# One load at a step: rows of x for the norms and the next tile's transposed x in the input projections of a hybrid decoder layer

## The chip, the core and the metric

The kernel runs on one core of a Trainium2 chip. The core has five engines with a queue of instructions each: TensorE (PE; its weight loads are shown apart, as PEld), VectorE (DVE), ScalarE (ACT), GpSimd (POOL) and SyncE (SP), which here issues nearly all transfers (DMAs) to the core's 16 DMA engines. An engine works its queue off in order, and an instruction waits until what it reads is there and the buffer that it writes is free. The metric is the device time of one execution in microseconds (us), as the median of several runs.

## The reference

One decoder layer on x of 2048 rows and 1024 columns, in float32: an input projection that feeds attention in a sliding window and a convolution group side by side, an output projection of both, and a gated feed-forward part. Every part has an RMS norm ahead of it and one behind.

```python
hn = rms_norm(h, mix_pre_g)                # 2048 x 1024
proj = hn @ w_in                           # 1024 x 1792: q, k, v, and u of the conv group
attn_out = sliding_window_attention(q, k, v, attn_sinks, rel_bias)   # window 128, 8 heads, 2 kv heads
conv_out = conformer_conv(u, ...)          # glu, causal depthwise conv of width 31, layer norm, swish, w_conv_pw
mixed = concatenate([attn_out, conv_out]) @ w_out
h = h + rms_norm(mixed, mix_post_g)
hn = rms_norm(h, ffn_pre_g)
ff = (silu(hn @ w_gate) * (hn @ w_up)) @ w_down      # 1024 -> 2816 -> 1024
h = h + rms_norm(ff, ffn_post_g)
```

`rms_norm(x, g)` divides each row by the root of its mean square: that root is what the rows of x are loaded for below.

## The kernel before

**Tiles and stages.** The 2048 rows are cut into four tiles of 512. A stage has a letter, and names of tiles in the profile carry it: `mm@A` is a PSUM bank of the input projections, `x@A` a tile of x, `hl@W` one of the output projection. A0 to A3 are the input projections of the four tiles, B attention, C the conv taps on DVE and their tail, U the product of `w_conv_pw` and `w_out`, W the output projection, H and F the norm and the gate/up matmuls of the feed-forward part, G the product with `w_down`, X the table of the relative-position bias. Float32 products are made of three fp32r matmuls: each operand is split into a high part (ACT, L127) and a rest (POOL, L129, or DVE, L94), and `three` multiplies high by high, high by rest and rest by high.

**Input projections.** One tile takes 14 units, one for each 128 of the 1792 columns of `w_in`. A unit loads its weights (`raw@A<-w_in`, L137, 512 KB; tile 0 stores the rests to `lo_in`, L131, and the other tiles load them from there, L126), splits them and runs 24 matmuls of 128x512 over the eight 128-row pieces of the transposed x (`hl@A`, `mid@A`, `chl@A`). After unit u, `step(u)` calls `hooks[u]`, if there is one: that is where the next tile is made ready.

**Getting the next tile ready.** Four functions do it. `load_x` (L247) loads the transposed x of a tile in four pieces of 512 KB (`x@A<-xT`, L252). `row_norms` (L261) loads rows of x, 128 at a time (`p@A<-x` or `hl@A<-x`, L266, 512 KB), has ACT square and sum each (`junk`, L267), and makes the reciprocal roots from the sums with one `rsqrt`, some small instructions on DVE and POOL (tiles `sm@A`). `norm_x` (hooks h2 and h3) turns the roots into a row that lies along the columns (`gb@A<-ident`, transposes into a bank, a copy by ACT), and `split_x` (h4 and h5) multiplies and splits x into the operands of the next tile. Tile 1 gets its own row norms during A0; those of tiles 2 and 3 are made together during A1. Tiles of x lie in a pool of four buffers (`x`), rows in pools of four (`p`) or eight (`hl`), weights in two (`raw`) and six (`w`). `yt` is a single buffer, used by the conv tail (`yt@C`) and then by the output projection (`yt@W`).

**What sets the order.** The units are written by a loop (`run`). Between its pieces, lanes (attention `lb`, taps `lc`, fold `lu`, output projection `lw` and others) are pumped by credits in proportion to the cost of each piece, so the order in which code is written mixes all stages. Behind that, a scheduler puts each engine's instructions in an order of its own: among what its model holds ready, the instruction written first goes first. Conv taps carry extra ties to the projections' instructions (`dve`), so that they keep pace. So a hook that is written differently can move instructions of other stages too, on every engine.

Of the kernel before, what the change touches and what calls it, by code (L numbers as in the profile page):

```python
# [17 lines left out]
AF = mybir.ActivationFunctionType  # L18
# [5 lines left out]
D = 1024  # L24
DFF = 2816
P = 128
T = 512
# [10 lines left out]
def layer_kernel(ctx, tc, x, xT, cols, rows, sinks, relb, onehot, w_in, w_pw, w_out, w_gate, w_up, w_down, out):  # L38
    nc = tc.nc
# [7 lines left out]
    lab = ["X0"]  # L47

    def nm(s):
        uid[0] += 1  # L50
        return f"{s}@{lab[0]}_{uid[0]}"
# [6 lines left out]
    def f4(tag, shape=(P, D)):  # L58
        return t_(tag, shape)
# [19 lines left out]
    act = nc.scalar.activation  # L79
# [64 lines left out]
    def rsqrt(ssq, n, mean_over, beside_taps=True):  # L144
        v = sm(n)
        y = sm(n)
        t = sm(n)
        vts(v, ssq, 1.0 / mean_over, EPS, ALU.mult, ALU.add)
        vts(y.bitcast(I32), v.bitcast(I32), 1, None, ALU.logical_shift_right)
        vts(y.bitcast(I32), y.bitcast(I32), -1, 0x5F3759DF, ALU.mult, ALU.add)  # L150
        for _ in range(3):
            if beside_taps:
                ptt(t, y, y, ALU.mult)
                ptt(t, t, v, ALU.mult)
                nc.gpsimd.tensor_scalar(t, t, -0.5, 1.5, ALU.mult, ALU.add)
# [45 lines left out]
    for i in range(4):  # L201
        xt = f4("x", (P, 2, T))
# [34 lines left out]
    junk = cst.tile([P, D], BF16, name="junk")  # L237
# [18 lines left out]

    rn = {}

    def row_norms(ts, tag):
        lab[0] = f"A{ts[0]}"  # L260
        n = 4 * len(ts)  # L261
        ssq = sm(n)
        for i in range(n):
            xt = f4(tag)
            r0 = ts[0] * T + i * P
            nc.sync.dma_start(xt, x[r0 : r0 + P])  # L266
            act(junk, xt, AF.Square, accum_out=ssq[:, i : i + 1])  # L267
# [16 lines left out]
    def norm_x(t, xs, acc):  # L284
        lab[0] = f"A{t}"
        bank_of = mm if t else ct
        if t:
            r = acc
        else:
            o = bank_of()  # L290
            for s in range(4):
                mat(o[:, s : s + 1], acc[:, s * P : (s + 1) * P], ones, start=True, stop=True)
            r = rsqrt(o[:, 0:4], 4, D, False)
        dg = f2("gb")
        for s in range(4):
            vts(dg[:, s * P : (s + 1) * P], ident, 0.0, r[:, s : s + 1], ALU.mult, ALU.add)
        yield
        lab[0] = f"A{t}"
        o = bank_of()
        for s in range(4):  # L300
            nc.tensor.transpose(o[:, s * P : (s + 1) * P], dg[:, s * P : (s + 1) * P], ident)
        rb = f2("gb")
        act(rb, o, AF.Copy)
        yield rb
# [1026 lines left out]
    H1, H2, H3, H4 = 0, 4, 7, 11  # L1331
# [28 lines left out]
    xa = {}  # L1360
# [8 lines left out]
    for t in range(NT):  # L1369
        hooks = {}  # L1370
        if t + 1 < NT:

            def h1(t=t + 1):
                xa[t] = load_x(t)

            def h3(t=t + 1):
                xa[t][2] = next(xa[t][2])

            def h4(t=t + 1):
                hn_a[t] = split_x(t, xa[t][0], xa[t][2], range(4))  # L1380
# [7 lines left out]
            def h2(t=t + 1):  # L1388
                xa[t] += [rn[t], norm_x(t, xa[t][0], rn[t])]
                next(xa[t][2])  # L1390
# [107 lines left out]
```

## Time and profile before

| | |
|---|---|
| median of 3 runs | 1985.41 us (1983.29 to 1989.4) |
| the profiled execution | 1988.67 us |
| its span, first to last instruction | 1986.6 us |
| mean granted clock of TensorE | 0.992 |
| PE busy | 1930.2 us (97%) |
| PEld busy | 1542.3 us (78%) |
| DVE busy | 1460.2 us (73%) |
| ACT busy | 955.2 us (48%) |
| POOL busy | 336.4 us (17%) |

The last matmul of the input projections starts at 484.5 us; the gate/up stage takes about 620 to 1010 us, the `w_down` products of the first half up to about 1340, and the second half of the feed-forward part the rest. In the rows of the profile, a time in brackets is idle time of the engine just before an instruction, followed by what ended it. `SPq` is an instruction of SP's queue that issues a DMA: its time is that of the issue, and the transfer lands later. In a row of a stretch stand, after its length, the busy time of PE, PEld, DVE, ACT and POOL with the number of instructions, then the granted clock of TensorE, the busy share of the DMA engines and GB/s.

### The profile page before, as it was taken

What the parts mean: (1) busy time and instruction counts of PE and PEld (TensorE: products, weight loads), DVE (VectorE), ACT (ScalarE), POOL (GpSimd) and SP (SyncE); (2) the same over time, 40 slices, a digit from 0 to 9 for tenths busy, and PEclk for the clock granted to TensorE, in tenths of its full rate; (3) what the DMA queues carried; (4) which work ended last, traced back from release to release, by engine and by line L of the source; (5) the groups of instructions that cost most, each with busy time, mean ns of one, the idle gap of its engine ahead of it and who ended that gap; (6) DMA issues with size and microseconds to landing.
All of it is one profiled execution on the core that took longest, in us unless ns stands there. A gap on an engine that the chain in (4) does not pass through costs nothing.

```text
span 1986.6 us, 26669 instructions
## 1 busy us (share of the span) xinstructions
PE 1930.2 (97%) x8730; PEld 1542.3 (78%) x8730; DVE 1460.2 (73%) x2578; ACT 955.2 (48%) x1878; POOL 336.4 (17%) x415
## 2 busy tenths in 40 slices
PE   8999999998999999899999999989999999999997
PEld 6777767776777778778888778768888888888886
DVE  5999969986875898888658975766666665455557
ACT  5455454436737633334355466556634433345443
POOL 4011111003121200000000110144423332311003
PEclk9999999999999999999999999989999999999999
DMA  8797757669659867885477788797844542466664
GB/s 312 253 316 234 228 176 242 213 198 306 203 191 353 290 216 237 285 267 181 154 236 251 266 302 282 270 315 244 289 149 165 170 164 81 143 232 194 210 196 144
DMA packets 229403, 454.56 MB, mean 229 GB/s; under 512 B 22632, under 2 KB 48400, under 8 KB 229264
## 3 DMA queue, kind: packets, MB, share of 16 engines
q1 hardware_dynamic: 211024, 426.64, 64.5%
q10 hardware_dynamic: 18240, 26.22, 3.6%
q8 instruction: 69, 1.13, 0.2%
q14 instruction: 70, 0.57, 0.1%
HBM read 331.65 MB, written 121.12 MB: 228 GB/s over the span
## 4 chain that ended last, share of the span: by engine, by line
PE 43%; DMA 10%; DVE 9%; issue 3%; POOL 2%; ACT 2%; SPq 1%; DVEq 0%; ACTq 0%; POOLq 0%
PE mm@F L85 29%; PE mm@G L85 12%; DVE fc@C L94 2%; PE tr@W L85 2%; DMA gb@F<-keeps 1%; DVE hl@G L94 1%; DMA mids<-fa@F 1%; DMA fa@G<-mids 1%; DMA td<-fc@G 1%; DVE w@F L94 1%; DMA fc@G<-w_down 1%; DMA wx@G<-w_down 1%; DVE fa@F L94 1%; DVE chl@F L94 1%; DMA mixT<-fc@C 1%
## 5 line engine op out<-in xcount | busy, mean ns | idle before, releaser
L94 DVE SCALAR_TENSOR_TENSOR fc@C<-glu@C,colt,fc@C 128x512 f32<-128x512 f32 x480 | 356.5, 760 | 2.9
L85 PE MATMUL mm@F<-hl@H,w@F 128*128 128x512 f32 x1056 | 253.0, 390 | 3.3 <-ACT mm@F L919 2.0
L85 PE MATMUL mm@G<-hl@G,hl@G 128*128 128x512 f32 x924 | 232.6, 397 | 11.2 <-ACT hl@G L792 7.7
L85 PEld LDWEIGHTS mm@F<-hl@H,w@F 128*128 128x128 f32 x1056 | 197.5, 188 | 46.3 <-ACT mm@F L919 3.7
L85 PEld LDWEIGHTS mm@G<-hl@G,hl@G 128*128 128x128 f32 x924 | 173.0, 190 | 51.7 <-ACT hl@G L792 9.0
L85 PE MATMUL mm@A<-hl@A,w@A 128*128 128x512 f32 x840 | 206.5, 395 | 4.2 <-ACT w@A L127 1.9
L792 ACT ACTIVATE w@F<-chl@F 128x512 fp32r<-128x512 f32 x220 | 135.4, 625 | 142.1 <-PE mm@F L85 131.5
L85 PE MATMUL mm@G<-w@G,hl@G 128*128 128x512 f32 x876 | 199.4, 389 | 0.0
L85 PEld LDWEIGHTS mm@G<-w@G,hl@G 128*128 128x128 f32 x876 | 164.4, 188 | 34.1
L85 PEld LDWEIGHTS mm@A<-hl@A,w@A 128*128 128x128 f32 x840 | 155.4, 188 | 42.2 <-ACT w@A L127 2.6
L94 DVE TENSOR_TENSOR w@F<-chl@F,w@F 128x512 fp32r<-128x512 f32 x198 | 144.8, 735 | 35.9 <-ACT w@F L792 35.3
L85 PE MATMUL mm@F<-ql@H,w@F 128*128 128x512 f32 x528 | 128.4, 391 | 9.2 <-ACT mm@F L1026 5.0
L85 PE MATMUL mm@F<-mid@H,w@F 128*128 128x512 f32 x528 | 131.7, 396 | 0.0
L85 PE MATMUL mm@F<-p@H,w@F 128*128 128x512 f32 x528 | 129.4, 390 | 0.0
L85 PE MATMUL mm@F<-x@H,w@F 128*128 128x512 f32 x528 | 125.7, 391 | 0.0
L85 PEld LDWEIGHTS mm@F<-ql@H,w@F 128*128 128x128 f32 x528 | 98.8, 188 | 31.6 <-ACT mm@F L1026 6.4
L494 POOL TENSOR_SCALAR_AFFINE_SELECT p@B<-p@B 128x512 f32<-128x512 f32 x62 | 57.6, 938 | 374.0 <-ACT p@B L492 372.7
L85 PEld LDWEIGHTS mm@F<-mid@H,w@F 128*128 128x128 f32 x528 | 100.0, 190 | 21.9 <-ACT fa@F L1047 0.5
L85 PEld LDWEIGHTS mm@F<-p@H,w@F 128*128 128x128 f32 x528 | 99.5, 188 | 21.0 <-ACT at@F L1040 0.2
L85 PEld LDWEIGHTS mm@F<-x@H,w@F 128*128 128x128 f32 x528 | 98.6, 188 | 21.5 <-issue 0.8
L127 ACT ACTIVATE w@A<-raw@A 128x512 fp32r<-128x512 f32 x110 | 67.4, 625 | 93.5 <-PE mm@A L85 54.8
L94 DVE TENSOR_TENSOR w@G<-raw@G,w@G 128x512 fp32r<-128x512 f32 x73 | 51.5, 705 | 68.1 <-ACT w@G L792 66.8
(302 smaller groups left out, 3300.6 us busy)
## 6 DMA issues: line engine op xcount, KB each, us to landing
mids<-fa@F SPq DMA_DIRECT2D x154, 256.0 KB, 2.8
raw@A<-w_in SPq DMA_DIRECT2D x55, 512.0 KB, 4.7
w@A<-lo_in SPq DMA_DIRECT2D x84, 256.0 KB, 3.6
fc@G<-mids SPq DMA_DIRECT2D x77, 256.0 KB, 3.5
fa@G<-mids SPq DMA_DIRECT2D x75, 256.0 KB, 4.6
gb@F<-keeps SPq DMA_DIRECT2D x72, 256.0 KB, 3.9
w@W<-fold SPq DMA_DIRECT2D x32, 512.0 KB, 5.1
chl@F<-w_gate SPq DMA_DIRECT2D x22, 512.0 KB, 4.1
```

The lines of the kernel that those rows point to most:

```text
L85: r = nc.tensor.matmul(*args, **kw)
L94: r = op(*args, **kw)
L127: act(w[:, 0], raw, AF.Copy)
L494: nc.gpsimd.affine_select(out=pg[:, kb].rearrange("p (i q) -> p i q", q=P), in_=pg[:, 1].rearrange("p (i q) -> p i q", q=P), compare_op=AL ...
L792: act(w[:, 0], x, AF.Copy)
```

## The change

The hooks load less at once. `load_x` takes a number of pieces and adds them to the tile's list; `row_norm` loads and squares one piece of 128 rows and makes the `rsqrt` of a tile with its fourth. Each tile has its own `rsqrt` now, with 4 values in place of 8 for tiles 2 and 3. During A0 the pieces of x go with steps 2, 3, 8 and 9, and the rows of tile 1 with steps 4 to 7, where all four of x stood at step 2 and all rows at step 4. During A1 the pieces of x go with steps 0, 1, 7 and 8, the rows of tile 2 with steps 2 to 5 and those of tile 3 with steps 6 to 9, where four of x stood at step 0 and eight rows at step 2; `h2` of tile 2 moves from step 7 to step 6. During A2 nothing changes: four of x at step H1.

```diff
-    def load_x(t):
+    def load_x(t, xs, n):
         lab[0] = f"A{t}"
-        xs = []
-        for i in range(4):
+        for i in range(len(xs), len(xs) + n):
             xt = f4("x", (P, 2, T))
             nc.sync.dma_start(xt, xT[2 * i : 2 * i + 2, :, t * T : (t + 1) * T].rearrange("c p t -> p c t"))
             xs.append(xt)
         started.add(f"x{t}")
-        return [xs]
...
-    def row_norms(ts, tag):
-        lab[0] = f"A{ts[0]}"
-        n = 4 * len(ts)
-        ssq = sm(n)
-        for i in range(n):
-            xt = f4(tag)
-            r0 = ts[0] * T + i * P
-            nc.sync.dma_start(xt, x[r0 : r0 + P])
-            act(junk, xt, AF.Square, accum_out=ssq[:, i : i + 1])
-        r = rsqrt(ssq, n, D)
-        for j, t in enumerate(ts):
-            rn[t] = r[:, 4 * j : 4 * j + 4]
+    def row_norm(t, i, tag):
+        lab[0] = f"A{t}"
+        if i == 0:
+            rn[t] = sm(4)
+        xt = f4(tag)
+        r0 = t * T + i * P
+        nc.sync.dma_start(xt, x[r0 : r0 + P])
+        act(junk, xt, AF.Square, accum_out=rn[t][:, i : i + 1])
+        if i == 3:
+            rn[t] = rsqrt(rn[t], 4, D)
...
-            def h1(t=t + 1):
-                xa[t] = load_x(t)
...
-            def h0(t=t + 1):
-                row_norms([t] if t == 1 else [2, 3], "p" if t == 1 else "hl")
+            xa[t + 1] = [[]]
+
+            def hx(n, t=t + 1):
+                load_x(t, xa[t][0], n)
+
+            def hr(t, i):
+                row_norm(t, i, "p" if t == 1 else "hl")
...
             if t == 0:
-                hooks = {2: h1, 4: h0, 8: h2, 10: h3, 11: h4, 12: h5}
+                hooks = {2: at_(hx, 1), 3: at_(hx, 1), 4: at_(hr, 1, 0), 5: at_(hr, 1, 1), 6: at_(hr, 1, 2), 7: at_(hr, 1, 3)}
+                hooks.update({8: lambda: (hx(1), h2()), 9: at_(hx, 1), 10: h3, 11: h4, 12: h5})
             elif t == 1:
-                hooks = {0: h1, 2: h0, 7: h2, 9: h3, 10: h4, 11: h5}
+                hooks = {0: at_(hx, 1), 1: at_(hx, 1)}
+                hooks.update({2 + i: at_(hr, 2, i) for i in range(4)})
+                hooks.update({6: lambda: (hr(3, 0), h2()), 7: lambda: (hx(1), hr(3, 1)), 8: lambda: (hx(1), hr(3, 2))})
+                hooks.update({9: lambda: (hr(3, 3), h3()), 10: h4, 11: h5})
             else:
-                hooks = {H1: h1, H2: h2, H3: h3, H4: h4}
+                hooks = {H1: at_(hx, 4), H2: h2, H3: h3, H4: h4}
```

Lines from L270 to L1365 of the kernel before are four lower in the changed one (L301 is L297 there). The scheduler's order of both kernels shows where instructions stand. On SP, in the first tile, the rows from the last pieces of x on, before (`lo_in` is a store of rests, `glu_scr` a store of the conv group's input, `glu@C` its load, `onehot` and `b_scr` belong to the bias table):

```order
L252 DMA x@A_46_339<-xT 128x2x512
L137 DMA raw@A_47_341<-w_in 128x1024
L131 DMA lo_in<-w@A_33_272 128x512
L616 DMA wx@U_366_2300<-w_pw 128x2x512
L131 DMA lo_in<-w@A_34_276 128x512
L137 DMA raw@A_55_395<-w_in 128x1024
L131 DMA lo_in<-w@A_48_343 128x512
L131 DMA lo_in<-w@A_49_347 128x512
L137 DMA raw@A_70_477<-w_in 128x1024
```

And the same place now:

```order
L137 DMA raw@A_44_335<-w_in 128x1024
L251 DMA x@A_100_710<-xT 128x2x512
L131 DMA lo_in<-w@A_33_272 128x512
L612 DMA wx@U_370_2319<-w_pw 128x2x512
L131 DMA lo_in<-w@A_34_276 128x512
L137 DMA raw@A_53_391<-w_in 128x1024
L131 DMA lo_in<-w@A_45_337 128x512
L131 DMA lo_in<-w@A_46_341 128x512
L137 DMA raw@A_62_446<-w_in 128x1024
```

The fourth piece of x stands behind the weights of unit 3 instead of ahead of them; the three pieces before it, and tile 1's rows, stand where they stood. Further on in the same tile, the loads of the bias table: before,

```order
L137 DMA raw@A_83_571<-w_in 128x1024
L356 DMA glu_scr<-fa@A_51_376 128x512
L131 DMA lo_in<-w@A_76_523 128x512
L131 DMA lo_in<-w@A_77_527 128x512
L137 DMA raw@A_90_621<-w_in 128x1024
L657 DMA b_scr<-fa@X_54_386 8x256
L538 DMA glu@C_88_614<-glu_scr 128x512
L131 DMA lo_in<-w@A_84_573 128x512
L131 DMA lo_in<-w@A_85_577 128x512
L137 DMA raw@A_96_670<-w_in 128x1024
L666 DMA mb@X_61_438<-b_scr 128x8x128
```

and now:

```order
L137 DMA raw@A_77_546<-w_in 128x1024
L534 DMA glu@C_82_589<-glu_scr 128x512
L131 DMA lo_in<-w@A_69_495 128x512
L653 DMA b_scr<-fa@X_51_380 8x256
L131 DMA lo_in<-w@A_70_499 128x512
L137 DMA raw@A_88_617<-w_in 128x1024
L662 DMA mb@X_59_434<-b_scr 128x8x128
```

`raw@A_83` and `raw@A_77` are the weights of the same unit (the eighth), `raw@A_90` and `raw@A_88` those of the ninth: the store to `b_scr` and the load of `mb@X` stand one unit of weights earlier.

On PE, at the end of the fourth tile's projections (`ct@C<-ident,yt@C` are the last transposes that read the conv tail's `yt`, `tr@B<-kz,ql@A` the scores of attention), before:

```order
L85 MATMUL mm@A_769_4719<-mid@A_504_3192,w@A_767_4713 128x512 x3
L85 MATMUL mm@A_769_4719<-mid@A_505_3196,w@A_767_4713 128x512 x2
L601 MATMUL ct@C_613_3763<-ident,yt@C_543_3430 128x128 x4
L85 MATMUL mm@A_769_4719<-mid@A_505_3196,w@A_767_4713 128x512
L85 MATMUL mm@A_769_4719<-mid@A_506_3200,w@A_767_4713 128x512 x3
L85 MATMUL mm@A_769_4719<-mid@A_507_3204,w@A_767_4713 128x512 x3
L85 MATMUL mm@A_769_4719<-hl@A_520_3295,w@A_768_4716 128x512 x3
L85 MATMUL mm@A_769_4719<-hl@A_521_3299,w@A_768_4716 128x512 x3
L85 MATMUL mm@A_769_4719<-hl@A_522_3303,w@A_768_4716 128x512 x3
L85 MATMUL mm@A_769_4719<-hl@A_523_3307,w@A_768_4716 128x512 x3
L85 MATMUL tr@B_783_4778<-kz,ql@A_752_4594 128x256
```

and now:

```order
L85 MATMUL mm@A_773_4738<-mid@A_508_3211,w@A_771_4732 128x512 x3
L85 MATMUL mm@A_773_4738<-mid@A_509_3215,w@A_771_4732 128x512 x3
L85 MATMUL mm@A_773_4738<-mid@A_510_3219,w@A_771_4732 128x512 x3
L597 MATMUL ct@C_617_3782<-ident,yt@C_547_3449 128x128 x4
L85 MATMUL mm@A_773_4738<-mid@A_511_3223,w@A_771_4732 128x512 x3
L85 MATMUL mm@A_773_4738<-hl@A_524_3314,w@A_772_4735 128x512 x3
L85 MATMUL mm@A_773_4738<-hl@A_525_3318,w@A_772_4735 128x512 x3
L85 MATMUL mm@A_773_4738<-hl@A_526_3322,w@A_772_4735 128x512 x3
L85 MATMUL mm@A_773_4738<-hl@A_527_3326,w@A_772_4735 128x512 x3
L85 MATMUL tr@B_787_4797<-kz,ql@A_756_4613 128x256
```

The transposes stand four matmuls later in the unit: 19 follow before the scores in the one, 15 in the other.

Orders differ in single rows up to the end of the gate/up stage, agree in the `w_down` products behind it, and differ at a few places after those. One such place on SP, in the gate/up stage (`chl@F<-w_gate` is a load of gate weights, `td<-` stores partial products of the first half, `gb@F<-keeps` loads kept products), before:

```order
L966 DMA raw@F_1357_8119<-w_up 128x1024
L968 DMA chl@F_1343_8002<-w_gate 128x1024
L1085 DMA td<-wx@G_1334_7956 128x512
L1085 DMA td<-fc@G_1336_7958 128x512
L1054 DMA mids_4750<-fa@F_1298_7717 128x512
L998 DMA gb@F_1339_7981<-keeps_4755 128x512
L1079 DMA wx@G_1367_8169<-w_down 128x512
```

and now:

```order
L962 DMA raw@F_1361_8138<-w_up 128x1024
L1081 DMA td<-wx@G_1338_7975 128x512
L1081 DMA td<-fc@G_1340_7977 128x512
L1075 DMA wx@G_1371_8188<-w_down 128x512
L964 DMA chl@F_1347_8021<-w_gate 128x1024
L1050 DMA mids_4769<-fa@F_1302_7736 128x512
L994 DMA gb@F_1343_8000<-keeps_4774 128x512
```

The gate weights stand behind two stores and a load of `w_down` that stood behind them.

More of the change, by code (lines that the diff above doesn't have):

```diff
@@ L1371, in layer_kernel, with h2 @@
         if t + 1 < NT:
-            def h1(t=t + 1):
-                xa[t] = load_x(t)
+            xa[t + 1] = [[]]
[3 more added lines that the diff above has]
+                row_norm(t, i, "p" if t == 1 else "hl")
+            def h2(t=t + 1):
+                xa[t] += [rn[t], norm_x(t, xa[t][0], rn[t])]
+                next(xa[t][2])
             def h3(t=t + 1):
@@ L1383, in h5 @@
                 hn_a[t] += split_x(t, xa[t][0], xa[t][2], range(4, KC))
-            def h0(t=t + 1):
-                row_norms([t] if t == 1 else [2, 3], "p" if t == 1 else "hl")
-            def h2(t=t + 1):
-                xa[t] += [rn[t], norm_x(t, xa[t][0], rn[t])]
-                next(xa[t][2])
+            at_ = lambda f, *a: lambda: f(*a)
             if t == 0:
-                hooks = {2: h1, 4: h0, 8: h2, 10: h3, 11: h4, 12: h5}
+                hooks = {2: at_(hx, 1), 3: at_(hx, 1), 4: at_(hr, 1, 0), 5: at_(hr, 1, 1), 6: at_(hr, 1, 2), 7: at_(hr, 1, 3)}
+                hooks.update({8: lambda: (hx(1), h2()), 9: at_(hx, 1), 10: h3, 11: h4, 12: h5})
             elif t == 1:
-                hooks = {0: h1, 2: h0, 7: h2, 9: h3, 10: h4, 11: h5}
+                hooks = {0: at_(hx, 1), 1: at_(hx, 1)}
+                hooks.update({2 + i: at_(hr, 2, i) for i in range(4)})
+                hooks.update({6: lambda: (hr(3, 0), h2()), 7: lambda: (hx(1), hr(3, 1)), 8: lambda: (hx(1), hr(3, 2))})
+                hooks.update({9: lambda: (hr(3, 3), h3()), 10: h4, 11: h5})
             else:
-                hooks = {H1: h1, H2: h2, H3: h3, H4: h4}
+                hooks = {H1: at_(hx, 4), H2: h2, H3: h3, H4: h4}
         run(mark(stage_a(t, hn_a[t], (lambda: lb.until(f"B{t-1}")) if t else (lambda: None), hooks,
```

## The prediction

> **What bounds the kernel now.** I read the page's first part, then the busy time of stretches, then the waits of PE and of its weight loads, then the order of time around each wait that the change can reach.
>
> ```profile
> span 1986.6 us, 26669 instructions
> PE 1930.2 (97%) x8730; PEld 1542.3 (78%) x8730; DVE 1460.2 (73%) x2578; ACT 955.2 (48%) x1878; POOL 336.4 (17%) x415
> ```
>
> PE is busy for 97% of the span, so at most 1986.6 − 1930.2 = 56.4 us is there to be won by removing waits. A busy PE may still be slower than its peak; the weight loads tell that. In a stretch with no stall they come to 16.57 of 20 us, so I read a stretch by how far it is under 16.57.
>
> ```profile
> core 0: us, PE busy (x) PEld busy (x) DVE busy (x) ACT busy (x) POOL busy (x), PEclk, DMA share, GB/s
> 20.00:40.00 20.00, 17.64 (x83) 14.23 (x82) 8.91 (x25) 9.20 (x17) 11.24 (x18) 1.00 0.88 330
> ...
> 480.00:500.00 20.00, 14.41 (x76) 11.75 (x75) 16.23 (x43) 7.53 (x17) 0.00 (x0) 0.83 0.93 322
> 800.00:820.00 20.00, 14.33 (x56) 11.00 (x55) 17.95 (x30) 3.79 (x7) 0.00 (x0) 0.91 0.78 264
> 860.00:880.00 20.00, 16.21 (x66) 12.94 (x65) 17.63 (x30) 6.17 (x12) 0.00 (x0) 0.93 0.78 249
> 1300.00:1320.00 20.00, 13.47 (x56) 10.24 (x55) 13.61 (x20) 11.12 (x27) 9.46 (x11) 0.85 1.04 356
> 1320.00:1340.00 20.00, 19.12 (x81) 15.28 (x81) 16.08 (x26) 6.81 (x14) 11.18 (x21) 0.90 0.83 273
> 1500.00:1520.00 20.00, 20.00 (x90) 16.57 (x89) 12.20 (x17) 8.99 (x16) 4.75 (x4) 1.00 0.40 132
> ```
>
> The holes are few, and the granted clock falls below 1 only where one is long. The waits name them:
>
> ```profile
> PE mm@G L85 <- ACT hl@G L792: 7.7, 3, 6.5
> PE tr@B L85 <- DVE sm@B L454: 5.6, 1, 5.6
> PE mm@F L85 <- ACT mm@F L1026: 5.0, 2, 3.8
> PE mm@F L85 <- ACT w@F L792: 4.0, 1, 4.0
> ...
> PEld tr@B L85 <- issue: 43.3, 95, 5.8
> ```
>
> Apart from these single waits, the largest item is the 43.3 us in which a weight load of attention (tr@B) stood without a releaser, in 95 places. So the kernel is bound by PE, and a change to loads pays only through these holes.
>
> **The change, part by part.**
>
> *Loads and squares of rows.* No DMA and no Square is added or removed, only placed elsewhere. Tile 1's stand at the same places on SP and ACT in both orders. Those of tiles 2 and 3 lie in this stretch:
>
> ```profile
> 93.00:117.00 24.00, 24.00 (x116) 18.53 (x115) 23.89 (x48) 13.54 (x26) 0.00 (x0) 1.00 0.98 366
> L267 ACT ACTIVATE junk<-hl@A 128x1024 bf16<-128x1024 f32 x8 | 8.4, 1054 | 8.3 <-DMA hl@A<-x 8.1
> 118.39 0.17 DVE L94 TENSOR_SCALAR sm@A<-sm@A 128x8 f32<-128x8 f32 x1
> 122.49 0.20 POOL L155 TENSOR_SCALAR sm@A<-sm@A 128x8 f32<-128x8 f32 x1
> ```
>
> The DMA engines are full there (0.98) and ACT waits 8.1 us for rows, but PE is busy 24.00 of 24.00 and the clock is 1.00: the burst is hidden under the matmuls, and spreading it wins 0. ACT is at 13.54 of 24 us, so a Square of 1.05 us in front of a weight conversion is hidden too. If that cover went, each of the 8 Squares could cost its 1.05 us, 8.4 in all; I take 0. The second rsqrt adds 3 small DVE instructions (3 × 0.17 = 0.5 us) and 12 on POOL (12 × 0.20 = 2.4 us). POOL does nothing in that stretch and DVE is off PE's path; what stands behind the DVE three are conv taps. Cost 0, at most 0.5.
>
> *The front of the first tile.* The fourth x load moves on SP behind the weight load of unit 3, and the loads for the bias table (one-hot, then b_scr and mb@X) move about one unit forward in SP's row.
>
> ```profile
> 20.39 0.46 SPq L137 DMA_DIRECT2D raw@A<-w_in  x1
> 29.68 0.60 ACT L303 ACTIVATE gb@A<-ct@A 128x512 f32<-128x512 f32 x1 [3.00 <-PE ct@A L301]
> 30.70 1.15 ACT L127 ACTIVATE w@A<-raw@A 128x512 fp32r<-128x512 f32 x2 [0.43 <-DMA raw@A<-w_in]
> 31.39 0.73 PE L85 MATMUL mm@A<-hl@A,w@A 128*128 128x512 f32 x2 [1.75 <-ACT w@A L127]
> ...
> 44.61 0.59 PE L85 MATMUL tr@X<-fa@X,rel 32*8 32x256 f32 x2 [0.48 <-DMA fa@X<-onehot]
> ...
> 60.03 1.96 PE L85 MATMUL tr@X<-mb@X,fa@X 128*128 128x512 f32 x4 [1.23 <-DMA mb@X<-b_scr]
> ```
>
> The weights of unit 3 were queued behind 512 KB of x; at the 330 GB/s of that stretch those are 524288 B / 330 GB/s = 1.6 us. Of these ACT can use 0.43 us: until 30.28 it was busy with the copy of ct@A. So PE's wait of 1.75 us shrinks by 0.43, between 0 and 1.6. The two waits for the table, 0.48 and 1.23 us, go, since both loads now stand ahead of a unit's weights and PE's order asks only 1 and 2 matmuls earlier (0.22 us each: 20 us / 90). Front: −0.43 − 0.48 − 1.23 = −2.1 us. What is late next is ACT: its third tanh stands one pair of weight conversions (1.15 us) earlier, so weights are made one unit less ahead. A unit of 24 matmuls lasts 24 × 0.222 = 5.3 us and ACT is busy 9.20 of 20 us in the stretch before, so I cost that at 0; lost cover would cost one pair, 1.15.
>
> *Places where attention interrupts projections.* In the order, PE goes into a 64-row matmul of another shape than the one before 105 times before and 98 times now; the amounts of each are the same. One such place in the trace, and the way back:
>
> ```profile
> 98.66 0.19 PEld L85 LDWEIGHTS tr@B<-kz,ql@A 64*128 64x128 f32 x2 [0.35 <-issue]
> 98.97 1.69 PEld L85 LDWEIGHTS mm@A<-mid@A,w@A 128*128 128x128 f32 x8
> ```
>
> Leaving out the one wait of 5.8, which is the stall at 485.9, one place costs (43.3 − 5.8) / 94 = 0.40 us. Seven fewer are −2.8 us; the bounds are 0 (if the load's gap hides behind the matmul before it) and −5.6 (twice). The row at 98.97, the way back, shows no wait. The Trainium skill, "TensorEngine Tiling (Array Packing)", section Key Properties, says that changing the tiling mode drains TensorE, in either direction; by it the way back would cost as much and this term would be −5.6. The trace shows a wait one way only, so the sum goes by −2.8.
>
> *End of the last projections.* Here the change costs.
>
> ```profile
> 479.92 0.60 PE L601 MATMUL ct@C<-ident,yt@C 128*128 128x128 f32 x4
> 480.55 0.37 SPq L705 DMA_DIRECT2D yt@W<-mixT  x1
> 483.66 0.55 DVE L94 TENSOR_SCALAR fc@C<-glu@C,colt 128x512 f32<-128x512 f32 x1 [7.43 <-DMA mixT<-fc@C]
> 490.69 2.19 ACT L708 ACTIVATE hl@W<-yt@W 128x512 fp32r<-128x512 f32 x4 [4.69 <-DMA yt@W<-mixT]
> 491.45 1.65 PE L85 MATMUL tr@B<-kz,ql@A 64*128 64x256 f32 x12 [5.59 <-DVE sm@B L454]
> 493.03 0.93 PEld L85 LDWEIGHTS mm@W<-w@W,hl@W 128*128 128x128 f32 x3 [0.22 <-ACT hl@W L708]
> ...
> L94 DVE SCALAR_TENSOR_TENSOR fc@C<-glu@C,colt,fc@C 128x512 f32<-128x512 f32 x480 | 356.5, 760 | 2.9
> ```
>
> The yt buffer is free after the transposes at 479.92, its load takes from 480.55 to 490.69, and the output projection starts at 493.03. In the new order 15 matmuls follow those transposes instead of 19 before the scores begin, so the load starts 4 × 0.22 = 0.9 us later against the end of the projections. DVE's chain (tap at 483.66, which waits for a store; scores' sum at 491.4) moves by as much: the transposes before that store stand 7 matmuls later (+1.6), and one conv tap of 0.76 us leaves its way. Both say about +0.9; bounds 0.8 and 1.6.
>
> *Sum.* −2.1 − 2.8 + 0.9 = −4.0 us on the profiled execution, whose own time is 1988.67 (2.07 outside the span of 1986.6). The median of the runs is 1985.41, 3.26 lower; the terms are waits of which each run has its share, so I forecast 1985.4 − 4.0 = 1981.4. That is −0.2%; a measurement of this kernel tells about 0.3% (6 us) from no change.
>
> **Rivals.**
>
> *A hole in the gate/up stage closes (faster).* In 620 to 1010 us the orders of SP, DVE and PE also differ in many single rows, though nothing there is in the diff; in the `w_down` products behind it they agree again, so the wait of 6.5 us there stays. The two holes of 4.0 and 3.8 us lie there. Against it: the loads that feed them, w_gate and gb@F, stand in the same sequence. If both close, 1981.4 − 7.8 = 1973.6; with the clock's loss in those stretches ((16.57 − 11.00 + 16.57 − 12.94) / 16.57 × 20 = 11.1 us in all) down to 1970.
>
> *A new hole opens in the gate/up stage (slower).* The place is near 833 us:
>
> ```profile
> 833.31 0.40 SPq L968 DMA_DIRECT2D chl@F<-w_gate  x1
> ...
> 837.65 0.42 SPq L998 DMA_DIRECT2D gb@F<-keeps  x1
> 838.43 0.68 DVE L94 TENSOR_TENSOR chl@F<-chl@F 128x512 f32<-128x512 f32 x1
> 838.89 0.33 SPq L1079 DMA_DIRECT2D wx@G<-w_down  x1
> 839.63 0.68 DVE L94 TENSOR_TENSOR chl@F<-chl@F,raw@F 128x512 f32<-128x512 f32 x1
> ```
>
> The new order puts this w_gate load behind two td stores and the w_down load that went out at 838.89. If that load still waits for its buffer, w_gate goes out at 839.3, 6.0 us late. DVE read it 5.1 us after the issue, so the hole is 5 to 6 us, from the point where it waits more than about 1 us. A hole of 6.5 us cost, with the clock at 0.85 and 0.90 in its two stretches, (2 × 16.57 − 10.24 − 15.28) / 16.57 × 20 = 9.2 us; so 1981.4 + 6 to 9.2, at its worst 1990.6, and above 1991.4 if the front's 2.1 us fail with it. Against it: DVE's rows were moved to suit, and the loads before it may go out sooner. Beside this: the Trainium skill, "TensorE: Matmul & The Clock Gate", section What's actually happening, has the clock at half after an idle window of about 3.4 us; by it every hole above that costs up to 1.7 us more. That is an estimate from that page. The rows agree so far that the stretches with such holes are the ones under 1.00.
>
> *The change doesn't do what it says.* The loads wait for buffers, and tile 1's keep their places on SP; then only the seven places matter, or not even those: 1985.
>
> **Chances.** Forecast 0.45, in which the terms leave 1979.5 to 1985: of it 0.05 below 1979.4 (−0.3%), 0.40 within. Hole closes 0.24, all faster. Hole opens 0.23, of it 0.17 above 1991.4. No effect 0.08, within. So faster 0.29, same 0.40 + 0.06 + 0.08 = 0.54, slower 0.17. The range runs from 1972 (most of the closing holes) to 1993.5 (the opened one with the front's gain lost).
>
> **What would show it.** Right: no wait of tr@X for onehot or mb@X; the wait for unit 3's weights shorter by 0.4; about 88 issue waits of tr@B at 0.40; the score wait near 485 at 6.5 in place of 5.6; the 100 to 120 us stretch still full of matmuls. Wrong: a wait above 3 us on mm@F or mm@A that is not in the list above, or one of the four gone.

## The result and the profile after

The changed kernel takes 1992.66 us (median of 7 runs, 1990.16 to 1997.18) against 1985.41 us (7 runs, 1982.06 to 1989.4) before: a ratio of 1.0037, 95% interval 1.0023 to 1.005. It is slower by 0.37%, some 7 us; I had forecast 4 us faster. The time lies inside the range, the sign was wrong.

The profiled execution of the changed kernel took 1997.18 us, the highest of its seven runs, and that of before 1988.67, so these two stand 8.5 us apart, a little more than the medians. From the page and the view of the cores, after:

```profile
span 1995.5 us, 26689 instructions
PE 1934.0 (97%) x8730; PEld 1547.7 (78%) x8730; DVE 1459.7 (73%) x2581; ACT 955.3 (48%) x1878; POOL 332.8 (17%) x427
core 0: 1995.5 us, clock 0.988
```

PE is busy 3.8 us longer for the same 8730 matmuls (1930.2 before), at a lower mean clock (0.992 before), and idle 61.5 us in place of 56.4. So about half of the 8.9 us of span is waiting and half is the same work at a slower clock.

Where it lies shows if the span is cut at the same matmuls. The main part of the gate/up stage, from one matmul near its start to one near its end, the same two and 1670 matmuls in both, is one row of the view of stretches. Before:

```profile
611.10:1009.80 398.70, 381.77 (x1670) 311.06 (x1669) 313.43 (x492) 174.15 (x309) 19.60 (x24) 0.99 0.72 241
```

and after:

```profile
610.60:1018.90 408.30, 386.57 (x1670) 315.87 (x1670) 312.96 (x495) 175.38 (x313) 18.98 (x24) 0.97 0.72 237
```

Up to the start of this stage the changed kernel is 0.5 us ahead. In it, 9.6 us are lost: 4.8 idle (408.30 − 386.57 = 21.7 against 16.9) and 4.8 more of busy time. Behind it the two differ by 0.2 us. **The whole loss lies in a stage in which the diff names nothing.** I had left that stage at no change.

The waits of PE in this stretch, after (in us: total, times, longest):

```profile
PE mm@F L85 <- ACT w@F L788: 6.5, 2, 3.8
PE mm@F L85 <- ACT mm@F L915: 5.1, 3, 2.4
PE mm@F L85 <- ACT fa@F L1043: 3.8, 2, 2.4
PE mm@F L85 <- ACT mm@F L1022: 3.1, 2, 2.1
PE mm@F L85 <- DVE gb@F L94: 2.5, 1, 2.5
```

Before, the largest were the 5.0 and 4.0 us shown in the prediction. No single wait has grown; there are more of middling size. Holes of PE over 1 us number nine here, 1.1 to 3.8 us long, with a sum of 20.0 us; before there were six with 13.4 us. Five of the nine are between 2.1 and 2.7 us long, a size that did not occur before.

What such a hole does to the granted clock, in short stretches around two of them, after. The first ends at 651.89 us (2.35 us long), the second at 853.58 (2.63):

```profile
649.00:652.00 3.00, 0.65 (x6) 0.41 (x5) 2.77 (x4) 2.86 (x6) 1.15 (x1) 1.00 0.87 295
652.00:655.00 3.00, 3.00 (x8) 2.40 (x9) 1.35 (x2) 2.52 (x5) 1.04 (x2) 0.55 0.64 160
655.00:658.00 3.00, 3.00 (x15) 2.41 (x15) 1.46 (x3) 1.20 (x3) 1.60 (x2) 0.88 0.14 53
```

```profile
850.00:853.50 3.50, 0.96 (x5) 0.46 (x3) 2.40 (x4) 1.12 (x3) 0.00 (x0) 1.00 0.97 363
853.50:857.00 3.50, 3.42 (x8) 2.76 (x9) 3.50 (x7) 1.55 (x4) 0.00 (x0) 0.53 0.78 266
```

The clock (third number from the right) drops to about half for some 3.4 us after the hole, so that 8 matmuls stand in 3.00 us where the next row has 15. In all, the trace has the clock at half for 6.8 us of this stage before and for 20.5 us after. Had PE been busy in all of the 13.7 us between them, that would cost 6.9 us of work; 4.8 were seen.

Two stretches that answer to those of the prediction, after:

```profile
93.00:117.00 24.00, 24.00 (x109) 17.44 (x108) 22.14 (x47) 12.43 (x23) 2.44 (x6) 1.00 0.97 366
480.00:500.00 20.00, 14.92 (x76) 11.98 (x76) 15.66 (x42) 9.94 (x19) 0.00 (x0) 0.83 1.04 366
```

93 to 117 us is still full of matmuls, with the DMA engines as busy (0.97) as before; but it holds 109 of them in place of 116. And the waits of the projections and of attention:

```profile
PE mm@A L85 <- ACT w@A L127: 1.4, 2, 1.2
PE tr@X L85 <- DMA mb@X<-b_scr: 1.1, 1, 1.1
PE tr@B L85 <- DVE sm@B L450: 5.0, 1, 5.0
PEld tr@B L85 <- issue: 43.0, 92, 5.2
```

One thing the hooks did not do: the loads were hardly spread. Tile 1's x and rows went out on SP from 11.8 to 22.2 us, from 11.0 to 20.0 before. Of the loads of the second tile's projections, these are the first row of tile 2 and the last two of tile 3, after:

```profile
92.60 0.33 SPq L263 DMA_DIRECT2D hl@A<-x  x1
105.36 1.60 SPq L263 DMA_DIRECT2D hl@A<-x  x2
```

and the first row and the last three before:

```profile
93.09 0.33 SPq L266 DMA_DIRECT2D hl@A<-x  x1
103.45 2.38 SPq L266 DMA_DIRECT2D hl@A<-x  x3
```

All eight rows and the four pieces of x between them go out within some 14 us in both kernels, though their hooks are spread over ten units now. What the change did move is the order of the instructions around them.

### The profile page after: what moved, and what is told of

Its sections match the earlier page's. It is cut to its first block, busy times and chain, and to the rows that moved or that the text cites. A ratio compares the mean times of both kernels' runs of the same rounds, so it can differ in the third digit from the quotient of the medians.

```text
span 1995.5 us, 26689 instructions
## 1 busy us (share of the span) xinstructions
PE 1934.0 (97%) x8730; PEld 1547.7 (78%) x8730; DVE 1459.7 (73%) x2581; ACT 955.3 (48%) x1878; POOL 332.8 (17%) x427
## 4 chain that ended last, share of the span: by engine, by line
PE 68%; DMA 13%; DVE 11%; issue 3%; POOL 2%; ACT 2%; SPq 0%; DVEq 0%; ACTq 0%; POOLq 0%
PE mm@F L85 30%; PE mm@G L85 13%; PE mm@A L85 13%; PE mm@W L85 4%; PE tr@B L85 4%; DVE fc@C L94 3%; PE tr@W L85 2%; DMA td<-fc@G 1%; DMA mids<-fa@F 1%; DMA fc@G<-w_down 1%; PE mm@U L85 1%; DMA gb@F<-keeps 1%; DVE hl@G L94 1%; DVE sm@G L94 1%; DVE w@F L94 1%
## 5 line engine op out<-in xcount | busy, mean ns | idle before, releaser
L85 PEld LDWEIGHTS mm@F<-p@H,w@F 128*128 128x128 f32 x528 | 101.8, 193 | 21.7
L490 POOL TENSOR_SCALAR_AFFINE_SELECT p@B<-p@B 128x512 f32<-128x512 f32 x62 | 52.5, 857 | 369.3 <-ACT p@B L488 367.8
```

The costliest lines, as they stand in the source:

```text
L85: r = nc.tensor.matmul(*args, **kw)
L490: nc.gpsimd.affine_select(out=pg[:, kb].rearrange("p (i q) -> p i q", q=P), in_=pg[:, 1].rearrange("p (i q) -> p i q", q=P), compare_op=AL ...
```

## The experiments

**The theories.** *Order:* the scheduler put the gate/up stage in another order because the hooks are written differently; the loads themselves cost nothing. *Loads:* the loads in their new places, or the second `rsqrt`, disturb something that runs on into that stage. *One place:* within the order theory, the w_gate load of the rival, behind two stores and a w_down load on SP, makes the loss.

To hold an order, the instructions of each engine from the start of the output projection on are tied in a chain along a table; a tie sets order alone and adds no wait:

```diff
+def pin(tc, start, orders):
+    traced = tc.nc.cur_bb.bb.instructions[start:]
+    for e, packed in orders.items():
+        mine = [i for i in traced if i.engine == getattr(mybir.EngineType, e)]
...
+        for a, b in zip(at[:-1].tolist(), at[1:].tolist()):
+            tc.add_manual_dep(mine[b], mine[a].name,
+                mybir.DependencyInfo(mybir.DependencyClass.NoSync, mybir.DependencyReason.DATA), reason="pinned order")
...
+    pin_from = len(nc.cur_bb.bb.instructions)      # behind the loop of the projections
...
+    pin(tc, pin_from, ORDERS)
```

**Crossing loads and order.** First the changed kernel with the order of before held from there on; then the kernel before with the order of after.

> The changed kernel up to the end of the input projections; from the output projection on, every engine's instructions are held in the order of the kernel before (order only, nothing waits more). Theory 'order': the loads as such are worth -0.5 us, and the 9.5 us that the gate/up stage lost come from the scheduler's new order there, so about 1985 us, within 1.5 us of before, gate/up stage (610 to 1010 us) back at about 398.7 us long. Rival 'loads': the spread loads leave buffers or transfers later and so slow the later stages whatever the order: about 1992.5 us, gate/up stage near 408 us.

> The kernel before up to the end of the input projections; from the output projection on, every engine in the order of the changed kernel. Theory 'order': about 1993 us, gate/up stage near 408 us. Rival 'loads': about 1985.5 us, gate/up stage near 399 us.

Measured: new loads in the old order 1985.16 us, ratio 0.999 (0.9981 to 0.9998); old loads in the new order 1997.68, ratio 1.0048 (1.0031 to 1.0065). The gate/up stage between the same matmuls, first of the new loads in the old order:

```profile
610.30:1008.80 398.50, 381.79 (x1670) 311.30 (x1670) 313.22 (x492) 174.00 (x309) 19.35 (x24) 0.99 0.72 241
```

and of the old loads in the new order:

```profile
610.40:1016.50 406.10, 384.20 (x1669) 313.28 (x1668) 312.47 (x494) 174.48 (x310) 19.05 (x24) 0.98 0.72 238
```

with the waits of PE in it:

```profile
PE mm@F L112 <- ACT w@F L819: 7.4, 2, 4.8
PE mm@F L112 <- ACT mm@F L946: 4.5, 3, 1.8
PE mm@F L112 <- ACT fa@F L1074: 3.9, 2, 2.8
```

The length goes with the order (398.5 as before, 406.1 nearly as after; two profiled executions of one kernel lie up to 2.6 us apart here, as shown below), whatever the loads do; the list of waits is that of the changed kernel, and its holes come at the same places (650.09, 706.50, 786.09, 817.19, 850.16 and 896.33 us, where the changed kernel has 651.89, 710.22, 790.38, 820.90, 853.58 and 898.71). The theory of the order holds, that of the loads falls. Neither kernel was run with its own order held; but the held orders take as long as the free ones (398.5 against 398.7, 406.1 against 408.3), so the ties show no cost here. The first of the two is also the best version of this study: clearly below the changed kernel, and some 2 us below the kernel before, which is less than the 0.3% that I set as told from no change.

**Half of the change at a time.** Hooks as changed during the first tile's projections only (a0), or during the second's only (a1):

```diff
 # a0: the second tile's hooks as before
+    hooks = {0: at_(hx, 4), 2: lambda: row_norms([2, 3], "hl"), 7: h2, 9: h3, 10: h4, 11: h5}
 # a1: the first tile's hooks as before
+    hooks = {2: at_(hx, 4), 4: lambda: row_norms([1], "p"), 8: h2, 10: h3, 11: h4, 12: h5}
```

> Only the first tile's hooks changed (tile 1's x and rows one at a step); rows of tiles 2 and 3 eight at once as before. Theory 'order': the gate/up stage gets a third order of its own, so its length comes out anywhere from 392 to 410 us; up to the end of the input projections within 1 us of before. Rival 'loads': a part of the 7 us, and together with the other half +7: if this half has none, 1985.4 us with the gate/up stage at 398.7.

> Only the second tile's hooks changed (rows of tiles 2 and 3 and x of tile 2 one at a step); tile 1's loads as before. Theory 'order': again an order of its own in the gate/up stage, its length anywhere from 392 to 410 us, not the complement of the other half. Rival 'loads': the two halves' differences add up to +7 us; eight rows spread are the larger part, so 1990 to 1993 us.

Measured: a0 1990.08 us, ratio 1.0016 (1.0005 to 1.0026); a1 2001.07, ratio 1.0072 (1.0057 to 1.0087). The halves don't add up: 0.16% and 0.72%, where both at once give 0.37%. The stage's row of a0:

```profile
608.30:1014.90 406.60, 387.29 (x1669) 315.75 (x1668) 312.03 (x494) 175.59 (x311) 19.21 (x24) 0.97 0.71 237
```

and of a1:

```profile
614.30:1022.10 407.80, 384.42 (x1670) 311.95 (x1669) 313.54 (x494) 175.12 (x311) 20.45 (x24) 0.99 0.71 237
```

Each half alone already brings the whole loss of this stage (+7.9 and +9.1); it is not a sum over what is edited. a0 makes up for part of it ahead of the stage (it starts at 608.3 in place of 611.1), and a1 loses 3.2 us more there. The same kernel a0, profiled a second time under the label that follows, took 1993.28 us in its one run, with the stage at 406.0:

> As the run with the first tile's hooks alone, but for a second look at its stages: input projections and output projection up to the gate/up stage 2 to 3 us shorter than before, gate/up stage 6 to 9 us longer, in the same places as in the first look.

**No load moved at all.** The kernel before with one `rsqrt` for tile 2 and one for tile 3, loads and hooks untouched:

```diff
-    row_norms([t] if t == 1 else [2, 3], "p" if t == 1 else "hl")
+    [row_norms([u], "p" if t == 1 else "hl") for u in ([t] if t == 1 else [2, 3])]
```

> The kernel before with one edit: tiles 2 and 3 get an rsqrt each, all loads where they were (3 small DVE and 12 small POOL instructions more, 2.9 us of their time in all, hidden). Theory 'order': the scheduler puts out another order of the gate/up stage for this too, so the time differs from before by several us although no load moved; holes of 2 us and more at new places. Rival 'loads': 1985 to 1988 us, as before, gate/up stage 398 to 400 us.

Measured: 1995.57 us, ratio 1.0041 (1.0029 to 1.0053).

```profile
614.50:1020.00 405.50, 385.66 (x1669) 314.41 (x1668) 312.74 (x493) 174.11 (x309) 19.34 (x24) 0.98 0.71 238
```

```profile
PE mm@F L85 <- ACT w@F L792: 6.8, 2, 3.9
PE mm@F L85 <- ACT mm@F L919: 4.5, 3, 2.3
PE mm@F L85 <- ACT mm@F L1026: 3.3, 2, 2.5
```

An edit that adds 3 small instructions on DVE and 12 on POOL and moves no load makes this stage 6.8 us longer, with holes at 653.63, 710.93, 791.36, 822.38, 854.76: the same ones as in the changed kernel. Another 3.4 us are lost ahead of the stage. The same kernel, profiled a second time under another label, with no order held, took 2001.31 us in its one run, with the stage at 408.1:

> A second look at the kernel with the two rsqrts and the scheduler's order: holes at the same places as in the first look (about 653, 711, 791, 822 and 854 us, 2.3 to 3.9 us each), which shows that they belong to the order and not to one execution.

Why the holes agree can be read from the traces. Taken by engine and by the names of tiles without buffer numbers, the instructions of this stretch stand in nearly one sequence in the changed kernel, a0, a1 and the kernel with two `rsqrt`. Of some 1668 matmuls, any two of these four have 1663 to 1668 in the same sequence, and each has 1450 to 1454 with the kernel before; of 298 DMAs on SP it is 291 to 298, against 250 to 252; of some 493 instructions on DVE 484 to 492, against 363 to 365. So the four edits did not get an order each, as was expected of the halves ("a third order of its own"). All four fell into the same other order: one alternative was met here, four times.

**The halves with the old order held.**

> Only the first tile's hooks changed, and from the output projection on the order of the kernel before. Theory 'order': 0.997 to 1.000 of before, since the edit left to the scheduler gave 1.0016 and two looks at it were 1.5 to 2.8 us shorter up to the gate/up stage. Rival 'part of the loss sits in the loads': 1.0016 or more, as without the held order.

> Only the second tile's hooks changed, and from the output projection on the order of the kernel before. Theory 'order': 1.000 to 1.0015 of before in place of 1.0072 (its input projections took 3 us longer in the one look). Rival 'loads': 1.005 or more.

Measured: a0 1989.09 us, ratio 1.0006 (0.9992 to 1.002); a1 1993.09, ratio 1.0022 (1.0008 to 1.0036). The stage in a0:

```profile
614.00:1013.40 399.40, 382.54 (x1669) 312.17 (x1668) 313.57 (x492) 174.44 (x309) 19.56 (x24) 0.99 0.72 241
```

and in a1:

```profile
614.80:1016.10 401.30, 383.15 (x1670) 312.59 (x1669) 314.67 (x492) 173.97 (x309) 19.74 (x24) 0.99 0.71 239
```

With the old order held, the stage takes 399.4 and 401.3 us again. Both ratios lie above what was expected of the theory of the order (at most 1.000 and 1.0015), though these limits lie inside the intervals; neither is as high as the rival's. What is left of a1 lies ahead of it: the last weight load of its projections stands at 487.1 us, against 484.2 before; that of the two separate `rsqrt` at 489.3. So these two edits on their own do cost some 3 to 5 us in the projections; both halves together show none (484.6). The projections vary by as much: this same weight load stands at 484.6 us in the changed kernel and at 479.5 in the next kernel below, whose projections are the same. But part of the loss has a cause in the traces. With a `rsqrt` of its own, tile 2's roots are made ready sooner, and the step that lays them along the columns (`gb@A<-ident`, at 126.99 us before) stands earlier on DVE. In the kernel with two `rsqrt`:

```profile
120.05 0.48 DVE L94 TENSOR_SCALAR gb@A<-ident,sm@A 128x128 f32<-128x128 f32 x2 [1.56 <-POOL sm@A L156]
122.15 0.94 PE L85 MATMUL tr@B<-kz,ql@A 64*128 64x256 f32 x11 [1.96 <-DVE sm@B L454]
```

DVE waits 1.56 us for the `rsqrt` on POOL, attention's sums stand behind that on DVE, and PE waits 1.96 us for these. Its second execution shows the same pair (1.56 and 2.0), a1 and a1 with the order held a smaller one (1.2 and 0.8 in both). In the changed kernel the step stands at 119.19 us and waits for nothing.

**One place on SP.** The changed kernel in its own order, all engines held, with the one w_gate load of the rival put back ahead of the stores, and the w_down load that stood before it put behind the load of kept products, as before the change:

```diff
 # SP's queue near 846 us
+chl@F <- w_gate
 td <- wx@G
 td <- fc@G
-wx@G <- w_down
-chl@F <- w_gate
 mids <- fa@F
 gb@F <- keeps
+wx@G <- w_down
```

> The changed kernel with its own order held on every engine, but for one place on SP in the gate/up stage: the seventh w_gate load goes out ahead of the two td stores and the w_down load again, as before the change. Theory 'SP queue at that place': the hole of 2.6 us at 853.6 us is gone or below 1 us, with it its window at half clock (1.7 us), so about 1988.5 to 1990 us against 1992.7 for the changed kernel. Rival 'DVE is the limit there': the hole stays at over 2 us, 1992.7 us.

Measured: 1996.27 us, ratio 1.0049 (1.0036 to 1.0061): nothing won. First the place in the changed kernel, in the order of time:

```profile
845.91 0.33 SPq L1075 DMA_DIRECT2D wx@G<-w_down  x1
846.34 0.38 SPq L964 DMA_DIRECT2D chl@F<-w_gate  x1
...
847.25 0.42 SPq L994 DMA_DIRECT2D gb@F<-keeps  x1
851.09 0.69 DVE L94 TENSOR_TENSOR chl@F<-chl@F 128x512 f32<-128x512 f32 x1 [2.24 <-DMA chl@F<-w_gate]
852.92 0.61 ACT L788 ACTIVATE w@F<-chl@F 128x512 fp32r<-128x512 f32 x1
853.58 1.14 PE L85 MATMUL mm@F<-ql@H,w@F 128*128 128x512 f32 x2 [2.63 <-ACT w@F L788]
```

then with the load put back, and SP's own wait there (830 to 850 us):

```profile
839.23 0.33 SPq L991 DMA_DIRECT2D chl@F<-w_gate  x1
841.09 0.88 SPq L1021 DMA_DIRECT2D gb@F<-keeps  x1
847.16 0.73 PE L112 MATMUL mm@F<-ql@H,w@F 128*128 128x512 f32 x2 [3.26 <-ACT w@F L815]
```

```profile
SPq L991 <- DVE w@F L121: 5.3, 1, 5.3
```

In the changed kernel the chain is as the rival had it: the load goes out late, DVE waits 2.24 us for it, ACT makes the weights, PE waits 2.63 us. With the load in its old place the hole is still there, 3.26 us: now SP itself stands for 5.3 us, in front of a load of this line whose buffer DVE has not yet let go. So the load's place on SP is not the cause alone. That the order of DVE, which frees the buffer, belongs to it is argued from this wait.

**Loads earlier in the old order.** New loads, old order held, with 27 loads of SP in this stage (`gb@F<-keeps`, w_gate, w_up) moved up to two places forward, past stores and w_down loads:

```diff
 # SP's queue, at 27 places of the gate/up stage (one of them)
+gb@F <- keeps
 td <- fc@G
 fc@G <- w_down
-gb@F <- keeps
```

> The changed loads, the order of the kernel before from the output projection on, and on SP 27 loads of kept products and of gate and up weights in the gate/up stage up to two places earlier, ahead of td stores, mids stores or w_down loads. Theory 'SP queue': these loads are what the holes wait for, so the waits of 4.0 and 3.8 us shrink by 1 to 2 us each and the time is 1978 to 1982 us, faster than before. Rival: what was passed (td stores, w_down loads) is late instead, DVE waits there, 1985 us or more.

Measured: 1995.51 us, ratio 1.0045 (1.0031 to 1.0059), and the stage at 410.4 us in place of 398.5. Loads that stand earlier made it 12 us longer: a miss for the idea that this stage waits because its loads stand late on SP. In front of its w_gate loads SP now stood 44.7 us, in 20 waits for DVE to let go of their buffers, against 23.7 us in 16 without the moves.

**One engine at a time.** The changed kernel with its own order held on four engines and the order of before on the fifth:

```diff
-pin(tc, pin_from, ORDERS_AFTER)
+pin(tc, pin_from, {**ORDERS_AFTER, "DVE": ORDERS_BEFORE["DVE"]})    # or PE, SP, Activation
```

> The changed kernel, held in its own order from the output projection on, but DVE held in the order of the kernel before. Theory 'DVE sets it' (DVE is the fullest engine beside PE in the gate/up stage, and the releases that SP waits for come from it): most of the loss comes back, 1985 to 1988.5 us, holes of 2 us and more fewer than the six of the changed kernel. Rival 'no engine alone' (each engine's order fits the others' of the same schedule): as slow as the changed kernel or slower, 1994 us and more.

> As above with PE alone in the order of before. Theory 'DVE sets it': no gain, 1993 us or more. Theory 'PE sets it' (the swaps of matmul groups in the gate/up stage ask for weights too early): 1985 to 1988.5 us. Rival 'no engine alone': 1994 us and more.

> As above with SP alone in the order of before. Theory 'DVE sets it': no gain, since what SP waits for is unchanged, 1993 us or more. Theory 'SP queue': 1985 to 1988.5 us. Rival 'no engine alone': 1994 us and more.

> As above with ACT alone in the order of before. ACT ends most holes (it waits for loads of kept products and has the weight conversions behind that wait). Theory 'ACT sets it': 1985 to 1988.5 us. Theory 'DVE sets it': 1993 us or more. Rival 'no engine alone': 1994 us and more.

| old order on | time, us | ratio (95%) |
|---|---|---|
| DVE | 2037.23 | 1.0245 (1.0232 to 1.0259) |
| SP | 2020.4 | 1.016 (1.0144 to 1.0175) |
| PE | 2012.43 | 1.0125 (1.011 to 1.014) |
| ACT | 2000.61 | 1.0062 (1.005 to 1.0073) |
| all five | 1985.16 | 0.999 (0.9981 to 0.9998) |

No engine's order on its own gives any of the loss back: against the 1.0037 (1.0023 to 1.005) of the changed kernel, DVE, SP and PE make it clearly worse, ACT by so little that the intervals touch, and all five together give back all of it. The orders of one schedule belong together, and the loss can't be put down to one queue. With DVE's order the stage takes 449.6 us, and over the whole span PE then waits above all for DVE:

```profile
PE mm@F L112 <- DVE gb@F L121: 24.2, 11, 7.3
```

**The gate/up stage in all of them**, in us, from one profiled execution each:

| order from the output projection on | lengths |
|---|---|
| that of before, also held under other loads (4 kernels) | 398.7, 398.5, 399.4, 401.3 |
| whatever the scheduler made after an edit (a0, a1, separate `rsqrt`, whole change; second executions of a0 and the separate `rsqrt`) | 406.6, 407.8, 405.5, 408.3; 406.0, 408.1 |
| that of after, held under the old loads | 406.1 |
| either order with loads of SP moved by hand | 412.3, 410.4 |
| that of after, one engine in that of before (ACT, PE, SP, DVE) | 414.3, 427.5, 435.5, 449.6 |

## Why the prediction was wrong

**The step that failed** stands under the rival of the closing hole, and the sum leans on it: that orders differ in many single rows of this stage "though nothing there is in the diff". The sum then gave the stage no term, so it put a new order at nothing without a price. It cost 9.6 us of the profiled executions, more than all terms of the sum together. The crossed pair shows that the order alone does it: 398.5 against 406.1 us.

**The rival of the opening hole** had the right stage, sign and size: it allowed up to 1990.6, or above 1991.4 with the front's gain gone, and 1992.66 came. Its mechanism was right at its place only in kind. The w_down load went out 7.0 us later than before (845.91 against 838.89) and the w_gate load behind it 13.0 later (846.34 against 833.31), so it was 6.0 us late, as worked out. But the hole was 2.63 us, not 5 to 6, and putting this load back gave nothing. So that its time came near is in part luck: what had to be priced was not one place but nine holes against six. I gave this rival 0.23, as I weighed one row that looked late against "DVE's rows were moved to suit"; both were arguments from an order about times.

**The closing hole** did not come: the waits of 4.0 and 5.0 us became 6.5 and 3.1 in the same list, with 5.1 and 3.8 new beside them.

**Loads and squares of rows, at 0:** the loads went out nearly as before, as the rival that the change doesn't do what it says had it (0.08), so no run tests what spreading them is worth. Nor does PE at 24.00 of 24.00 in 93 to 117 us show that nothing was lost there. By the prediction's own measure, the weight loads, it has 17.44 us in place of 18.53, and (18.53 − 17.44) / 16.57 × 20 = 1.3 us of work are missing. From 101 to 111 us attention's scores go in between the projections' matmuls seven times in place of three, and their weight loads wait 1.7 us in place of 0.6. That is the order of PE, not the loads. **The second `rsqrt`, at most 0.5,** was under-priced in part: on its own it made PE wait 1.96 us, through POOL and DVE, though DVE was taken to be off PE's path; in the whole change that wait did not appear.

**Front of the first tile, −2.1:** part of it came. The wait for the one-hot load is gone. The waits for converted weights in the first 110 us come to 1.4 us, the longest 1.2, where that for unit 3's alone was 1.75: 0.5 us gone, near the 0.43 expected. But with the old loads and the new order, where this front is that of before, they come to 1.4 us as well, so the change isn't shown to have done it. The 1.23 us for `mb@X` did not go in the changed kernel's trace (1.1 left), though it did in that of the new loads in the old order, which starts alike. A wait of 0.6 us for ACT's `hl@A` is new (0.9 there). All waits of PE in these 110 us come to 6.7 us before, 6.2 in the changed kernel and 5.4 there: −0.5 and −1.3.

**Places where attention interrupts projections, −2.8:** it brought nothing that can be seen. The row has 92 waits in place of 95, not 88: 43.0 us, without its longest (43.0 − 5.2) / 91 = 0.415 us each. The price was right, and the sum of the waits the same: 1.1 us came in at 101 to 111 us, and about as much went elsewhere. The order told of 7 fewer entries into such matmuls, but the trace's count of weight loads that wait is not the order's count of entries. The estimate by the rule of the Trainium skill ("TensorEngine Tiling (Array Packing)", Key Properties: a change of mode drains TensorE), −5.6, was farther off; no row shows a drain on the way back.

**End of the last projections, +0.9:** wrong in sign. The wait before the scores fell from 5.6 to 5.0 us, and the stretch from the last projection to the gate/up stage from 126.9 to 126.0. The transposes that stand four matmuls later in the order still fed DVE in time. Both of the rows that I had taken for agreement were counts of matmuls in an order, so one argument, not two.

**The three terms together:** −4.0 was forecast for what the diff touches. New loads in the old order stood about 2 us below before, at the edge of what these runs can tell (0.9981 to 0.9998), so the sign was right and the size about half. The traces point the same way: the last matmul of the projections starts at 479.7 to 484.8 us in the eight kernels that have the whole change there (481.7 on average), and at 484.5 and 485.4 in the two that have the projections of before.

**What stays open.** Which feature of the new order makes its holes: the swaps show only that it is not one engine's order. And why the scheduler, after four different edits, leaves the order of before for one that is 7 to 10 us longer here; the code of the stage is written in the same sequence in all of them. Since the four got nearly the same order, they can't tell whether orders made anew tend to be worse than that of before. The rest of the 3 us that a1 loses in the projections was seen, not explained.

## What to carry to other kernels

Where a scheduler sets the order, an edit is two changes: what it does, and the new order of everything behind it, which here cost 7 to 10 us in a stretch that starts some 400 us behind the edit (611 us, where the second tile's projections end near 193), while the edit itself gave 2. Cross the two (new code with the old order held, old code with the new order) before you judge an edit; this takes two kernels and settles it. "Orders differ there" deserves a term of its own, and not a zero, even where the diff names nothing. Whether a new order of a stage of which PE is busy for 96% is likelier to lose than to win can't be told from the one that was met here. And look in the trace whether the loads go out where the hooks now stand: here they went out as bunched as before.

## What the runs showed of the hardware

Holes shorter than 3 us can cost more than their own length. After holes of 2.35, 2.53 and 2.63 us the clock stood near half for some 3.4 us; after one of 1.70 us, and after two others of 2.13 and 2.41 us, it stayed at 1.00. The stretches behind the 1.70, the 2.13 and the 2.41 us, after:

```profile
631.50:635.00 3.50, 3.23 (x14) 2.70 (x15) 1.32 (x3) 2.17 (x5) 0.00 (x0) 1.00 0.97 316
790.30:794.00 3.70, 3.62 (x16) 2.99 (x17) 2.56 (x5) 1.10 (x3) 0.00 (x0) 1.00 1.05 342
898.60:902.00 3.40, 3.29 (x14) 2.73 (x15) 2.75 (x5) 2.26 (x6) 0.00 (x0) 1.00 0.00 0
```

Even a hole of 1.07 us, at 641.29, had a piece at half clock behind it. What sorts them is a grid. In this stage of the changed kernel the clock falls to half at 642.07, 652.31, 710.34, 819.56 and 853.70 us, and these times lie 3, 17, 32 and 10 times 3.41 us apart; half clock lasts for one such piece, for two from 819.56 us on. Cut at this grid, the piece ahead of the fall at 642.07, the piece at half clock, and the pieces that hold all of the 1.70 us and most of the 2.41:

```profile
638.66:642.07 3.41, 1.59 (x9) 1.09 (x8) 3.22 (x5) 3.17 (x7) 1.27 (x1) 1.00 1.03 375
642.07:645.49 3.42, 3.42 (x9) 2.65 (x8) 1.49 (x3) 2.34 (x5) 2.01 (x2) 0.50 1.10 341
628.42:631.83 3.41, 1.72 (x9) 1.10 (x7) 0.95 (x2) 1.72 (x4) 0.00 (x0) 1.00 1.05 399
894.66:898.07 3.41, 1.64 (x8) 1.02 (x6) 2.06 (x4) 0.53 (x1) 0.00 (x0) 1.00 0.74 270
```

Of the pieces of this stage at full clock, the five that half clock followed have PE busy for 0.79 to 1.59 us, and all others for 1.64 us or more. So in this trace a hole also costs the clock behind it where it leaves a piece of the grid less than about half busy, and where it falls on the grid decides that as much as its length. The edge is not sharp: in the trace of before, pieces with 1.49 and 1.57 us stayed at full clock.

The Trainium skill, "TensorE: Matmul & The Clock Gate", section What's actually happening, gives one idle window of about 3.4 us as what brings the slow clock: the length of the pieces agrees with the trace, but a piece in which PE was busy for 1.59 us was already enough here. In the prediction I had priced a hole of 5 to 6 us with its clock and left the smaller ones at their length.
